# Strassen operands of an encoder layer: transposing the four plain blocks and forming the sums from transposed blocks

## The chip, the core and the metric

The kernel runs on one core of one Trainium2 chip. The metric is the device time of one execution in microseconds (us); the time of a kernel is the median over several runs. The engines of the core are named PE (TensorE, matmul; its weight loads are PEld), DVE (VectorE), ACT (ScalarE), POOL (GpSimd) and SP (SyncE). SBUF is the core's working memory, PSUM the small memory into which PE writes.

## The reference

One layer of an encoder: 1024 tokens, width 1024, float32 in and out.

```
x += 1/2 * post(SwiGLU_1(pre(x)))                      macaron half-step FFN
x += post(W_out [ norm(NA heads) | norm(dilated heads) ])  parallel head groups
     sharing one combined q/k/v projection of pre(x)
x += 1/2 * post(SwiGLU_2(pre(x)))                      macaron half-step FFN
...
def swiglu(x, w_gate, w_up, w_down):
    return (jax.nn.silu(x @ w_gate) * (x @ w_up)) @ w_down
```

`pre` and `post` are root-mean-square norms with a gain. The hidden width of the two SwiGLU networks is 2816. The large products have pre(x) on the left: the gates and ups of ffn1, q/k/v, and the gates and ups of ffn2.

## The kernel before

**Products.** Each float32 operand is split into a high and a low part of a shorter format (`fp32r`): hi is a cast on ACT, lo is the difference on DVE. A product is then three matmuls (`mm3`, L251 to L253). Above this lies one level of Strassen's scheme in Winograd's form: the left operand, pre(x) transposed, is cut into four blocks of 512x512, and seven products are made of the left blocks and sums A11, S2, S1, S4, A12, S3, A22 with the right ones (B and T). The left sums are S1 = A21 + A22, S2 = S1 - A11, S3 = A11 - A21, S4 = A12 - S2.

**The left operands.** The class `Operand` makes these seven in three places of the program: before ffn1, before the q/k/v projection and before ffn2. The tokens come in eight tiles of 128. Of tiles 0 to 3 come A11 (left half of the columns) and A12 (right half); of tiles 4 to 7 come A22, S1, S2, S3 and S4, whose sums take tile t and tile t-4. For each tile, `squares` sums the squares (ACT, L151), `scale` makes the factor on DVE (L134 to L144) and `tile` writes the normalised tile `xn` (L200). Tiles 0 to 3 are saved to memory by a DMA of POOL (L203) and loaded again as `x1` (L217) when their partner is in work. `sums` forms the four sums in the natural layout into `s` (L223). Each of the 28 pieces of a place then goes through `transpose_in`: four transposes on PE into `trp` (L159; two PSUM buffers), the cast hi by ACT (L160) and the subtraction lo by DVE (L161).

**Buffers.** `xn` has 3 buffers at ffn1 and 2 at the other places (`c.xn`); `x1` and `s` have 2 at ffn1 and 1 at the others (`c.deep`). In the last two places `squares` uses the next `xn` buffer as its throw-away output, so it too waits for that buffer.

**What sets the order.** The pieces are fed in between the matmuls of another product: after every six matmuls, `Ctx.step` takes one entry of `c.sums` (norms and sums) and one of `c.steps` (a piece); what is left is done in a row by `flush`. PE keeps this order as it is written. ACT and DVE keep it only at the head of ffn1; elsewhere a scheduler sets the order of ACT, DVE, POOL and SP. During ffn1 and ffn2 the pieces lie between the first products of the gate and up weights, which need A11 and A12 alone ("early" pairs: 9 at ffn1, 10 at ffn2; their weights `graw` are split into `whi` and `wlo`, L344 and L345). Then `begin` prepares the right operands of the first pair: `traw` (T2) and `wraw` are weight sums (L432 to L434, DVE), split at L344 and L345; the first product of the run of all seven is S2 x T2. In the early pairs `sg` is the activated product (L528, ACT), `s` at L363 the kept copy of the A11 product. At the q/k/v projection the pieces for tiles 4 to 7 lie within the product for v, whose output is copied to `vt` (L1357) and whose weights are cast at L600. The residual stream x is read and written by POOL's DMAs at L705 and L709 between the norms.

Of the kernel before, what the change touches and what calls it, by code (L numbers as in the profile page):

```python
# [10 lines left out]
F32 = mybir.dt.float32  # L11
# [8 lines left out]
P, T = 128, 512  # L20
# [8 lines left out]
A11, S2, S1, S4, A12, S3, A22 = range(7)  # L29
# [124 lines left out]
def transpose_in(c, x, hi, lo, tag="tr", pool=None):  # L154

    nc = c.nc
    ps = (pool or c.pst).tile([P, 4, P], F32, tag=tag, name="trp")
    for j in range(4):
        nc.tensor.transpose(ps[:, j, :], x[:, j * P:(j + 1) * P], c.ident)  # L159
    nc.scalar.copy(hi, ps)  # L160
    nc.vector.tensor_sub(lo, ps, hi.bitcast(F32))  # L161


class Operand:
# [9 lines left out]
    def second(self):  # L174
        for b in (S1, S2, S3, S4, A22):
            self.x[b] = [self.c.xb.tile([P, 4, T], F32R, tag=f"x{b}{i}", name=f"x{b}{i}") for i in range(2)]
# [19 lines left out]
    def tile(self, t, x, xn, r):  # L196
        c, nc = self.c, self.c.nc
        if xn is None:
            xn = c.xp.tile([P, D], F32, tag="xn", name="xn", bufs=c.xn)
        nc.vector.scalar_tensor_tensor(xn, x, r, self.gain, op0=ALU.mult, op1=ALU.mult)  # L200
        a1, a2 = xn[:, :T], xn[:, T:]
        if t < 4:
            nc.gpsimd.dma_start(self.saved[t], xn)  # L203
            self.parts[t] = deque(((A11, a1), (A12, a2)))
        else:
            self.wait.append((t, a1, a2))
            self.sums()

    def sums(self):

        c, nc = self.c, self.c.nc
        if not self.wait or self.open == c.deep:
            return
        self.open += 1
        t, a1, a2 = self.wait.popleft()
        x1 = c.xp.tile([P, D], F32, tag="x1", name="x1", bufs=c.deep)
        nc.gpsimd.dma_start(x1, self.saved[t - 4])  # L217
        s = c.xp.tile([P, 4, T], F32, tag="s", name="s", bufs=c.deep)
        a11, a12 = x1[:, :T], x1[:, T:]
        s1, s2, s3, s4 = [s[:, i, :] for i in range(4)]  # L220
        add, sub = nc.vector.tensor_add, nc.vector.tensor_sub
        for f, *args in ((add, s1, a1, a2), (sub, s2, s1, a11), (sub, s3, a11, a1), (sub, s4, a12, s2)):
            c.sums.append(lambda f=f, args=args: f(*args))  # L223
        parts = deque(((A22, a2), (S1, s1), (S2, s2), (S3, s3), (S4, s4)))
        c.sums.append(lambda: self.parts.__setitem__(t, parts))

    def put(self, t):

# [3 lines left out]
    def one(self, t):  # L232
        while not self.parts.get(t):
            self.c.sums.popleft()()
        b, src = self.parts[t].popleft()
        cols = slice(t % 4 * P, t % 4 * P + P)
        transpose_in(self.c, src, *[h[:, :, cols] for h in self.x[b]])
        if t >= 4 and not self.parts[t]:
            self.open -= 1
            self.sums()  # L240
# [82 lines left out]
class PairGemm:  # L323
# [17 lines left out]
    def split(self, raw, tag, pool=None):  # L341
        c, nc = self.c, self.c.nc
        hi, lo = [(pool or c.wr).tile(list(raw.shape), F32R, tag=tag + p, name="w" + p) for p in ("hi", "lo")]
        nc.scalar.copy(hi, raw)  # L344
        nc.vector.tensor_sub(lo, raw, hi.bitcast(F32))  # L345
        return hi, lo
# [73 lines left out]
    def prepare(self, b):  # L420


        nc = self.c.nc
        if b >= self.n:
            return [lambda: None] * 4
        r, w = self.raw.pop(b), self.w.setdefault(b, {})
        t2 = self.c.wt.tile([P, 1, T], F32, tag="t", name="traw")

        def direct():
            if b >= self.early:  # L430
                w["g"] = self.split(r[:, 0:4:3, :], "g")
            nc.vector.tensor_sub(r[:, 0:2], r[:, 1:3], r[:, 0:2])  # L432
            nc.vector.tensor_sub(t2[:, 0], r[:, 2], r[:, 0])  # L433
            nc.vector.tensor_sub(r[:, 3], r[:, 3], t2[:, 0])  # L434

        def second():
            w[T2] = self.split(t2, "t", self.c.wt)

        def sums():
            w[T1] = self.split(r[:, 0:2, :], "m")  # L440

        def rest():
            w[B22] = self.split(r[:, 2:4, :], "n")
            self.fetch(b + 2)
        return direct, second, sums, rest
# [11 lines left out]
    def run(self, final=None):  # L457
# [3 lines left out]
        for b in range(self.n):  # L461
            w, early = self.w.pop(b), b < self.early
            direct, second, sums, rest = self.prepare(b + 1)
            if early:
                s1 = sp.tile([P, T], F32, tag="s1", name="s1")
# [30 lines left out]
            c22 = c.cp.tile([P, T], F32, tag="g2", name="c22", bufs=3)  # L496
            nc.vector.tensor_add(c22, d, v)
            sums()
            self.mm(a, w[B22], 0, S4, True)
            self.sink.second(b, a, u2 if early else None)  # L500
# [13 lines left out]
class GatePairs:  # L514
# [7 lines left out]
    def first(self, b, ps, keep, s1=None):  # L522
        c, nc = self.c, self.c.nc
        sg = c.sp.tile([P, T], F32, tag="s1", name="sg") if keep else self.tile()
        if s1 is not None:
            nc.vector.tensor_add(sg, ps, s1)
            ps = sg
        nc.scalar.activation(sg, ps, AF.Silu)  # L528
        self.sg[b] = sg
        if keep:  # L530
            self.sg[b] = d = c.dr.tile([P, T], F32, name="sgd")
            nc.gpsimd.dma_start(d, sg)
# [133 lines left out]
class Finish:  # L666
# [33 lines left out]
    def rest(self, ts, h):  # L700

        c, nc = self.c, self.c.nc
        xs = [c.xp.tile([P, D], F32, tag="x", name="x") for t in ts]
        for t, x in zip(ts, xs):
            nc.gpsimd.dma_start(x, self.src[t])  # L705

        def add(t, x):
            nc.vector.scalar_tensor_tensor(x, h(t), self.r[t], x, op0=ALU.mult, op1=ALU.add)
            nc.gpsimd.dma_start(self.dst[t], x)  # L709
        c.sums.extend([lambda: None] * 2 + [lambda t=t, x=x: add(t, x) for t, x in zip(ts, xs)])  # L710
        if self.op is not None:
            c.sums.append(lambda: self.op.norm(ts, xs))
# [884 lines left out]
```

## Time and profile before

| what | value |
|---|---|
| time, median of 3 runs | 1975.63 us (1974.63 to 1976.17) |
| profiled execution | span 1973.4 us; the page shows no other time for it |
| granted TensorE clock, mean | 0.977 |
| traffic to and from memory | 203 GB/s over the span |

The rows of five stretches show the three places. Columns: start and end, length, busy us and count of PE, PEld, DVE, ACT and POOL, the granted clock (1.00 is full speed), the busy share of the DMA engines and GB/s.

```profile
50.00:75.00 25.00, 25.00 (x134) 20.65 (x134) 23.43 (x43) 15.18 (x25) 4.87 (x9) 1.00 0.58 194
85.40:100.00 14.60, 13.54 (x65) 11.02 (x64) 8.96 (x12) 6.95 (x11) 2.16 (x4) 1.00 0.90 351
635.00:725.00 90.00, 84.72 (x390) 67.77 (x389) 72.51 (x132) 44.40 (x73) 15.64 (x29) 1.00 0.70 244
1300.00:1345.00 45.00, 39.55 (x182) 31.67 (x181) 33.32 (x63) 25.58 (x40) 10.26 (x19) 0.95 0.83 299
1345.00:1376.00 31.00, 27.29 (x122) 22.04 (x121) 21.26 (x36) 11.76 (x20) 3.76 (x7) 0.85 0.40 137
```

In the first PE never stops; in the last two, at ffn2, it stands for 5.45 us of 45 and 3.71 us of 31, and the clock is below full speed. In the timeline a row is start, duration, engine, line, operation, tiles, and in brackets the idle time before it with what released it.

### The profile page before, as it was taken

The page shows a single profiled execution, that of the slowest core. Times are in us where ns is not written, and L with a number is a line of the kernel's source. Part 1 is how long each engine was busy: PE and PEld are TensorE (multiplying, and loading weights), DVE is VectorE, ACT ScalarE, POOL GpSimd, SP SyncE. Part 2 cuts the span into 40 slices and gives each one's busy share as a digit, 9 for nine tenths or more (in the row PEclk, how much of TensorE's full clock was granted, in tenths as well). Part 3 has the DMA queues.
Part 4 walks back from the last instruction along what each step waited for, and adds up shares of the span by engine and source line. Part 5 has one row for each costly group of instructions (what it writes and reads, how often), then busy time and mean ns, then how long its engine had stood idle before and what let it go on. Part 6 is the DMA issues. An engine that isn't in the chain of part 4 may idle for free. (4 is left out here: it accounts for less than half of the span.)

```text
span 1973.4 us, 25565 instructions
## 1 busy us (share of the span) xinstructions
PE 1878.4 (95%) x9044; PEld 1566.3 (79%) x9044; DVE 1329.0 (67%) x2235; ACT 807.0 (41%) x1463; POOL 323.3 (16%) x520
## 2 busy tenths in 40 slices
PE   5999999999999989999899788998999999999997
PEld 4888888887888868778898777876888888878886
DVE  5778776764656775577565565676788777745567
ACT  4522233333534455133676555454222333335333
POOL 2101111111000123323444220021011111110000
PEclk8999999999999999999999799998999999999999
DMA  6655565555876767868999881375456665467664
GB/s 234 216 170 176 180 231 203 202 192 208 292 251 204 255 232 254 243 214 244 207 190 159 144 164 32 132 271 193 160 178 204 234 225 192 172 220 234 202 220 143
DMA packets 170433, 398.63 MB, mean 202 GB/s; under 512 B 20080, under 2 KB 41504, under 8 KB 170304
## 3 DMA queue, kind: packets, MB, share of 16 engines
q1 hardware_dynamic: 118800, 222.34, 36.1%
q0 software_dynamic: 50640, 172.55, 27.6%
q10 hardware_dynamic: 864, 2.10, 0.3%
q8 instruction: 71, 1.16, 0.2%
q14 instruction: 58, 0.48, 0.1%
HBM read 272.55 MB, written 127.26 MB: 203 GB/s over the span
## 5 line engine op out<-in xcount | busy, mean ns | idle before, releaser
L251 PE MATMUL mmp<-x,whi 128*128 128x512 f32 (+1 forms) x1464 | 580.9, 397 | 7.6 <-ACT whi L344 3.5
L253 PE MATMUL mmp<-x,wlo 128*128 128x512 f32 (+1 forms) x1464 | 576.5, 394 | 1.1 <-DVE wlo L345 1.1
L252 PE MATMUL mmp<-x,whi 128*128 128x512 f32 (+1 forms) x1464 | 576.1, 394 | 0.6 <-DVE x L161 0.5
L251 PEld LDWEIGHTS mmp<-x,whi 128*128 128x128 f32 x1464 | 278.8, 190 | 67.4 <-ACT whi L344 4.2
L253 PEld LDWEIGHTS mmp<-x,wlo 128*128 128x128 f32 x1464 | 278.7, 190 | 62.2 <-DVE wlo L345 1.9
L252 PEld LDWEIGHTS mmp<-x,whi 128*128 128x128 f32 x1464 | 278.9, 191 | 59.8 <-DVE x L161 1.5
L601 DVE TENSOR_TENSOR pw<-praw,pw 128x1024 fp32r<-128x1024 f32 (+1 forms) x182 | 198.9, 1139 | 128.1 <-ACT pw L600 128.0
L600 ACT CAST pw<-praw 128x1024 fp32r<-128x1024 f32 (+1 forms) x182 | 168.4, 981 | 215.6 <-PE accp L253 173.5
L252 PE MATMUL accp<-pw 128*128 128x512 f32 x616 | 241.7, 392 | 4.9 <-DVE pw L601 4.9
L251 PE MATMUL accp<-pw 128*128 128x512 f32 x616 | 241.9, 393 | 2.6 <-ACT pw L600 2.6
L253 PE MATMUL accp<-pw 128*128 128x512 f32 x616 | 241.2, 391 | 0.0
L344 ACT CAST whi<-wraw 128x1024 fp32r<-128x1024 f32 x129 | 135.3, 1050 | 248.6 <-PE mmp L252 223.2
L345 DVE TENSOR_TENSOR wlo<-wraw,whi 128x1024 fp32r<-128x1024 f32 x129 | 157.7, 1224 | 23.8 <-ACT whi L344 23.6
L252 PEld LDWEIGHTS accp<-pw 128*128 128x128 f32 x616 | 116.4, 189 | 30.1 <-DVE pw L601 6.4
L251 PEld LDWEIGHTS accp<-pw 128*128 128x128 f32 x616 | 116.4, 189 | 27.5 <-ACT pw L600 3.5
L253 PEld LDWEIGHTS accp<-pw 128*128 128x128 f32 x616 | 116.4, 189 | 24.2
L549 POOL DMA_DIRECT2D g<-sg x44 | 23.8, 540 | 473.3 <-DVE sg L542 285.8
L363 ACT COPY s<-mmp 128x512 f32<-128x512 f32 x52 | 30.5, 586 | 149.8 <-PE mmp L253 148.1
L505 DVE TENSOR_TENSOR c<-mmp,u 128x512 f32<-128x512 f32 x52 | 35.9, 691 | 81.2 <-PE mmp L253 80.9
L161 DVE TENSOR_TENSOR x<-trp,x 128x512 fp32r<-128x512 f32 x84 | 57.2, 687 | 35.6 <-ACT x L160 35.6
L344 ACT CAST whi<-traw 128x512 fp32r<-128x512 f32 x52 | 32.3, 621 | 117.1 <-DVE traw L433 58.4
L432 DVE TENSOR_TENSOR wraw<-wraw 128x1024 f32<-128x1024 f32 x52 | 63.7, 1224 | 23.5 <-DMA wraw<-in_wqk_dram 12.6
(223 smaller groups left out, 2760.9 us busy)
## 6 DMA issues: line engine op xcount, KB each, us to landing
praw<-g SPq DMA_DIRECT2D x70, 512.0 KB
wraw<-in_wg_dram SPq DMA_DIRECT2D x44, 512.0 KB
wraw<-in_wu_dram SPq DMA_DIRECT2D x44, 512.0 KB
tr<-in_wd_dram SPq DMA_DIRECT2D x44, 512.0 KB
g<-sg POOLq DMA_DIRECT2D x88, 256.0 KB, 3.4
ts<-tr POOLq DMA_DIRECT2D x22, 1024.0 KB, 4.7
praw<-ts SPq DMA_DIRECT2D x88, 256.0 KB
praw<-in_wd_dram SPq DMA_DIRECT2D x66, 256.0 KB
```

What stands on the lines that cost most here:

```text
L161: nc.vector.tensor_sub(lo, ps, hi.bitcast(F32))
L251: nc.tensor.matmul(out, ahi, bhi, start=start, stop=False, skip_group_check=go_on)
L252: nc.tensor.matmul(out, ahi, blo, start=False, stop=False, skip_group_check=go_on)
L253: nc.tensor.matmul(out, alo, bhi, start=False, stop=stop, skip_group_check=go_on)
L344: nc.scalar.copy(hi, raw)
L345: nc.vector.tensor_sub(lo, raw, hi.bitcast(F32))
L363: self.c.nc.scalar.copy(s, ps)
L432: nc.vector.tensor_sub(r[:, 0:2], r[:, 1:3], r[:, 0:2])
L505: nc.vector.tensor_add(c21, d, u2)
L549: nc.gpsimd.dma_start(self.g[A12 if b % 2 else A11][b // 2], g)
L600: nc.scalar.copy(w[:, side, 0, :m], raw[:, :m])
L601: nc.vector.tensor_sub(w[:, side, 1, :m], raw[:, :m], w[:, side, 0, :m].bitcast(F32))
```

## The change

Only plain blocks are transposed: A11 and A12 of tiles 0 to 3, A22 and A21 (the two halves) of tiles 4 to 7. A place has 16 groups of four transposes in place of 28. A transposed block is copied back by ACT over the half of `xn` that it came from, so that `xn` then holds transposed blocks; the save of tiles 0 to 3 comes after the second half's copy, and `x1` is loaded transposed. The sums are formed from transposed blocks: S1 and S3 read A21 from PSUM, S2 and S4 read SBUF; their hi and lo are split from `s` in SBUF. A tile of the second half is now five steps: `right` (transpose A22, split, copy back), `left` (transpose A21, S1 and S3), `first` (split S1, form S2), `second` (split S2, form S4), `rest` (split S4 and S3). The number of DVE's operations and of DMAs stays as it is; ACT has 12 copies more per place. Lines behind `Operand` stand 39 further down.

```diff
--- before.py
+++ after.py
@@ -198,13 +198,35 @@
         if xn is None:
             xn = c.xp.tile([P, D], F32, tag="xn", name="xn", bufs=c.xn)
         nc.vector.scalar_tensor_tensor(xn, x, r, self.gain, op0=ALU.mult, op1=ALU.mult)
-        a1, a2 = xn[:, :T], xn[:, T:]
         if t < 4:
-            nc.gpsimd.dma_start(self.saved[t], xn)
-            self.parts[t] = deque(((A11, a1), (A12, a2)))
+            self.parts[t] = deque([lambda: self.plain(t, xn, 0, A11), lambda: self.plain(t, xn, 1, A12)])
         else:
-            self.wait.append((t, a1, a2))
+            self.wait.append((t, xn))
             self.sums()
+
+    def cols(self, t, b):
+        return [h[:, :, t % 4 * P:t % 4 * P + P] for h in self.x[b]]
+
+    def split(self, t, b, src):
+        nc = self.c.nc
+        hi, lo = self.cols(t, b)
+        nc.scalar.copy(hi, src)
+        nc.vector.tensor_sub(lo, src, hi.bitcast(F32))
+
+    def turned(self, xn, half):
+
+        c, ps = self.c, self.c.pst.tile([P, 4, P], F32, tag="tr", name="trp")
+        for j in range(4):
+            c.nc.tensor.transpose(ps[:, j, :], xn[:, half * T + j * P:half * T + j * P + P], c.ident)
+        return ps, xn[:, half * T:half * T + T].rearrange("p (k c) -> p k c", k=4)
+
+    def plain(self, t, xn, half, b):
+
+        ps, back = self.turned(xn, half)
+        self.split(t, b, ps)
+        self.c.nc.scalar.copy(back, ps)
+        if half:
+            self.c.nc.gpsimd.dma_start(self.saved[t], xn)
 
     def sums(self):
 
@@ -212,17 +234,36 @@
         if not self.wait or self.open == c.deep:
             return
         self.open += 1
-        t, a1, a2 = self.wait.popleft()
+        t, xn = self.wait.popleft()
         x1 = c.xp.tile([P, D], F32, tag="x1", name="x1", bufs=c.deep)
         nc.gpsimd.dma_start(x1, self.saved[t - 4])
-        s = c.xp.tile([P, 4, T], F32, tag="s", name="s", bufs=c.deep)
-        a11, a12 = x1[:, :T], x1[:, T:]
-        s1, s2, s3, s4 = [s[:, i, :] for i in range(4)]
+        s = c.xp.tile([P, 4, 4, P], F32, tag="s", name="s", bufs=c.deep)
+        a11, a12 = [x1[:, i * T:i * T + T].rearrange("p (k c) -> p k c", k=4) for i in range(2)]
+        s1, s2, s3, s4 = [s[:, i] for i in range(4)]
         add, sub = nc.vector.tensor_add, nc.vector.tensor_sub
-        for f, *args in ((add, s1, a1, a2), (sub, s2, s1, a11), (sub, s3, a11, a1), (sub, s4, a12, s2)):
-            c.sums.append(lambda f=f, args=args: f(*args))
-        parts = deque(((A22, a2), (S1, s1), (S2, s2), (S3, s3), (S4, s4)))
-        c.sums.append(lambda: self.parts.__setitem__(t, parts))
+
+        def right():
+            ps, back = self.turned(xn, 1)
+            self.split(t, A22, ps)
+            nc.scalar.copy(back, ps)
+
+        def left():
+            ps, _ = self.turned(xn, 0)
+            add(s1, ps, xn[:, T:].rearrange("p (k c) -> p k c", k=4))
+            sub(s3, a11, ps)
+
+        def first():
+            self.split(t, S1, s1)
+            sub(s2, s1, a11)
+
+        def second():
+            self.split(t, S2, s2)
+            sub(s4, a12, s2)
+
+        def rest():
+            self.split(t, S4, s4)
+            self.split(t, S3, s3)
+        self.parts[t] = deque((right, left, first, second, rest))
 
     def put(self, t):
 
@@ -232,9 +273,7 @@
     def one(self, t):
         while not self.parts.get(t):
             self.c.sums.popleft()()
-        b, src = self.parts[t].popleft()
-        cols = slice(t % 4 * P, t % 4 * P + P)
-        transpose_in(self.c, src, *[h[:, :, cols] for h in self.x[b]])
+        self.parts[t].popleft()()
         if t >= 4 and not self.parts[t]:
             self.open -= 1
             self.sums()
```

How the built orders move, at three places. First ACT at the end of the early pairs of ffn1; the line L344 (L383 after the change) casts weights, L160 (L213) casts the left operands, L528 (L567) is the activation of an early product. Before:

```order
L160 CAST x_177<-trp 128x4x128
L160 CAST x_179<-trp 128x4x128
L363 COPY s_885<-mmp 128x512
L528 ACTIVATE sg<-mmp 128x512
L344 CAST whi<-traw 128x512
L528 ACTIVATE sg<-mmp 128x512
L344 CAST whi<-wraw 128x1024 x2
L344 CAST whi<-traw 128x512
L344 CAST whi<-wraw 128x1024
```

The same place with the change:

```order
L213 CAST x_173<-s 128x4x128
L213 CAST x_177<-s 128x4x128
L213 CAST x_175<-s 128x4x128
L402 COPY s_837<-mmp 128x512
L213 CAST x_179<-s 128x4x128
L567 ACTIVATE sg<-mmp 128x512 x2
L383 CAST whi<-wraw 128x1024
L383 CAST whi<-traw 128x512
```

The two casts of weights have changed places, and both now stand behind the last two activations, where the cast of `traw` stood between them.

Second POOL at the head of the norms of ffn2; L203 (L229) saves the normalised tile, L705 and L709 (L744 and L748) read and write the residual stream, L217 (L239) loads a saved tile again. Before:

```order
L705 DMA x<-x_2_95 128x1024
L705 DMA x<-x_3_96 128x1024
L203 DMA xn_0_10909<-xn 128x1024
L203 DMA xn_1_10910<-xn 128x1024
L709 DMA x_2_103<-x 128x1024
L709 DMA x_3_104<-x 128x1024
L217 DMA x_11580<-xn_0_10909 128x1024
L203 DMA xn_2_10911<-xn 128x1024
```

With the change:

```order
L744 DMA x<-x_2_95 128x1024
L744 DMA x<-x_3_96 128x1024
L748 DMA x_2_103<-x 128x1024
L748 DMA x_3_104<-x 128x1024
L229 DMA xn_0_10813<-xn 128x1024
L229 DMA xn_1_10814<-xn 128x1024
L239 DMA x_11492<-xn_0_10813 128x1024
L744 DMA x<-x_4_97 128x1024
L744 DMA x<-x_5_98 128x1024
L229 DMA xn_2_10815<-xn 128x1024
L229 DMA xn_3_10816<-xn 128x1024
```

The saves of tiles 0 and 1 have moved behind the two writes of x, and those of tiles 2 and 3 behind two reads.

Third DVE at the second half of the tiles of ffn2; L432 (L471) is the first weight sum of `begin`, which waits for a weight's DMA, L134 starts the norm of the next two tiles. Before:

```order
L161 TENSOR_TENSOR x_11429<-trp,x_11428 128x4x128
L223 TENSOR_TENSOR s<-s,x_11728 128x512
L223 TENSOR_TENSOR s<-x_11728,xn 128x512
L223 TENSOR_TENSOR s<-x_11728,s 128x512
L161 TENSOR_TENSOR x_11431<-trp,x_11430 128x4x128
L134 TENSOR_SCALAR v<-ss 128x2
L432 TENSOR_TENSOR wraw<-wraw 128x1024
L135 TENSOR_SCALAR y<-v 128x2
L161 TENSOR_TENSOR x_11423<-trp,x_11422 128x4x128
L136 TENSOR_SCALAR y<-y 128x2
L345 TENSOR_TENSOR wlo<-graw,whi 128x1024
```

With the change:

```order
L214 TENSOR_TENSOR x_11343<-trp,x_11342 128x4x128
L471 TENSOR_TENSOR wraw<-wraw 128x1024
L252 TENSOR_TENSOR s<-trp,xn 128x512
L253 TENSOR_TENSOR s<-x_11626,trp 128x512
L257 TENSOR_TENSOR s<-s,x_11626 128x512
L214 TENSOR_TENSOR x_11335<-s,x_11334 128x4x128
L384 TENSOR_TENSOR wlo<-graw,whi 128x1024
L261 TENSOR_TENSOR s<-x_11626,s 128x512
L214 TENSOR_TENSOR x_11337<-s,x_11336 128x4x128
L134 TENSOR_SCALAR v<-ss 128x2
```

Before, the four sums of tile 5 stood ahead of L432; now all four and a low half of early weights stand behind it.

## The prediction

> **What bounds the kernel now.** I read the page first, then the groups of the trace that touch the tile `trp`, then the order of time around each place where the operands are made.
>
> ```profile
> span 1973.4 us, 25565 instructions
> PE 1878.4 (95%) x9044; PEld 1566.3 (79%) x9044; DVE 1329.0 (67%) x2235; ACT 807.0 (41%) x1463; POOL 323.3 (16%) x520
> ```
>
> PE is busy for 95% of the span, and the other engines have room on average. So an instruction taken from PE shortens the span by its own length, unless PE then reaches something that is not ready. The question is which of the two happens at each of the three places (before ffn1, before the q/k/v projection, before ffn2).
>
> ```profile
> L159 PE MATMUL trp<-ident,s x192: 269/272/477, 53.3 to 1371.0; 128*128 128x128 f32 x192
> L159 PE MATMUL trp<-ident,xn x144: 270/273/475, 11.9 to 1365.3; 128*128 128x128 f32 x144
> ```
>
> These are the transposes: 192 of sums, 144 of plain blocks. The durations (min, median, max in ns) overlap in the pipeline, so the price is read from the starts:
>
> ```profile
> 53.29 0.60 PE L159 MATMUL trp<-ident,s 128*128 128x128 f32 x4
> ...
> 55.14 0.60 PE L159 MATMUL trp<-ident,s 128*128 128x128 f32 x4
> ...
> 1376.30 0.40 PE L251 MATMUL mmp<-x,whi 128*128 128x512 f32 x1
> ...
> 1377.68 0.40 PE L251 MATMUL mmp<-x,whi 128*128 128x512 f32 x1
> ```
>
> From one group of four to the next, with six matmuls after the first, PE takes 55.14 - 53.29 = 1.85 us; six matmuls alone take 1377.68 - 1376.30 = 1.38 us. A group costs 0.47 us; over several such pairs I take **0.45 us**.
>
> **What the change removes.** Per place, tiles 0 to 3 keep 2 groups each; tiles 4 to 7 fall from 5 groups to 2. That is 28 groups before and 16 after, 12 fewer: 12 x 0.45 = **5.4 us per place, 16.2 us in all**. ACT gets 12 copies back from `trp` per place, of about 0.57 us, and DVE does as many subtractions as before:
>
> ```profile
> L160 ACT CAST x<-trp x84: 565/586/605, 13.8 to 1371.5; 128x512 fp32r<-128x512 f32 x84
> L161 DVE TENSOR_TENSOR x<-trp,x 128x512 fp32r<-128x512 f32 x84 | 57.2, 687 | 35.6 <-ACT x L160 35.6
> L223 DVE TENSOR_TENSOR s<-xn x12: 680/686/693, 47.9 to 1363.5; 128x512 f32<-128x512 f32 x12
> ```
>
> A subtraction that reads PSUM takes 687 ns, a sum in SBUF 686 ns: where the operand lies changes nothing, so the work that moves between them is costed at nothing. The 36 copies are 36 x 0.57 = 20 us of ACT; PE covers them, except where a cast that PE waits for stands behind one. I now follow the changed orders place by place.
>
> **Place 1 (ffn1).** Five transposes in a flush before the last early pair made PE wait, and this wait goes:
>
> ```profile
> 87.50 0.66 PE L159 MATMUL trp<-ident,s 128*128 128x128 f32 x4 [1.06 <-DVE x L161]
> 93.82 0.60 ACT L528 ACTIVATE sg<-mmp 128x512 f32<-128x512 f32 x1 [2.19 <-PE mmp L253]
> 94.31 0.61 ACT L344 CAST whi<-traw 128x512 fp32r<-128x512 f32 x1
> 96.61 0.60 ACT L528 ACTIVATE sg<-mmp 128x512 f32<-128x512 f32 x1 [1.69 <-issue]
> 97.11 1.99 ACT L344 CAST whi<-wraw 128x1024 fp32r<-128x1024 f32 x2
> ```
>
> What is late next is the product S2 x T2, which starts without a wait at 96.37. Its T2 cast stands between the last two activations of `sg` and is done at 94.92. In the changed order ACT does both activations, then the 1024-wide cast, and only then T2's. The last `sg` waits for the matmuls that end just ahead of the product, so PE waits for the tail of it (0.50), a 1024-wide cast (1.05, less 0.1 of overlap) and T2's cast (0.62): 2.1 us. The low half then needs two subtractions on DVE, and its matmul comes about 1.0 later: -3.1 in all. At the head of the program a copy back stands ahead of the second cast (0.5), and the fourth `xn` (3 buffers) now waits for the save of tile 0, which the diff puts behind the copy back of the second half. The save starts near 22.8, and
>
> ```profile
> DMA to landing us min/median/max: 2.9/4.1/7.0
> 27.46 0.56 POOL L203 DMA_DIRECT2D xn<-xn  x1 [7.88 <-DVE xn L200]
> ```
>
> the first row (landing of the saves) puts it at 26.9, where this `xn` was written just before its save at 27.46: no slack, 0.3. After a wait the clock can fall:
>
> ```profile
> 1339.73 0.40 PE L253 MATMUL mmp<-x,wlo 128*128 128x512 f32 x1
> 1343.24 0.66 PE L159 MATMUL trp<-ident,s 128*128 128x128 f32 x4 [3.12 <-DVE x L161]
> ...
> 1344.38 0.63 PE L253 MATMUL mmp<-x,wlo 128*128 128x512 f32 x1
> 1344.81 0.63 PE L251 MATMUL mmp<-x,whi 128*128 128x512 f32 x1
> 722.53 0.50 PE L251 MATMUL mmp<-x,whi 128*128 128x512 f32 x1 [1.66 <-ACT whi L344]
> 1344.00:1348.00 4.00, 4.00 (x14) 3.23 (x13) 3.76 (x13) 1.69 (x3) 0.54 (x1) 0.58 0.35 131
> ```
>
> After a wait of 3.12 us the matmuls are 0.43 apart in place of 0.23, for about eight of them: 8 x 0.20 = 1.6 us lost, at a granted clock of 0.58; the wait of 1.66 us is followed by a matmul of 0.50, near the usual 0.40 and far from 0.63. A wait of 3.1 in two parts lies between: 0 to 1.6, I take 1.0. **Place 1: 5.4 + 1.06 - 3.1 - 0.8 - 1.0 = +1.6 us.**
>
> The Trainium skill, "TensorE: Matmul & The Clock Gate", Part 1, says that the gate halves the clock after an idle window of about 3.4 us, and that the window runs free of the kernel. The rows above agree for 3.12 (0.58) and for 1.66. Taken strictly, a wait in two parts of 2.1 and 1.0 never empties a window, and the sum would be 1.0 better.
>
> **Place 2 (q/k/v).** Here the flush stands at the end of V's product:
>
> ```profile
> 715.13 0.66 PE L159 MATMUL trp<-ident,s 128*128 128x128 f32 x4 [0.67 <-DVE x L161]
> 720.95 0.59 ACT L1357 COPY vt<-accp 128x512 f32<-128x512 f32 x1 [0.85 <-PE accp L253]
> 721.43 1.99 ACT L344 CAST whi<-graw 128x1024 fp32r<-128x1024 f32 x2
> ```
>
> The 0.67 goes. PE then stands at 722.53 (row above) for `whi`, which ACT casts behind the last `vt` copy. In the changed order the last tile's casts of S3 and S4 stand ahead of these, so of the 2.0 us that PE saves on the last tiles (4.4 groups) only 0.7 arrives: -1.3. The first weight cast of V's S2 pass is moved behind the activation of another tile: bounds 0 and the 2.0 of two casts (1.99 above), I take 1.0, the middle, as no row is nearer. Cold clock: 0 to 1.6, I take 0.5. **Place 2: 5.4 + 0.67 - 1.3 - 1.0 - 0.5 = +3.3 us.**
>
> **Place 3 (ffn2).** Here the old kernel waits longest, and the new one gets new waits.
>
> ```profile
> 1364.90 0.63 PE L159 MATMUL trp<-ident,xn 128*128 128x128 f32 x4 [1.48 <-DVE x L161]
> ...
> 1367.81 1.96 PE L159 MATMUL trp<-ident,s 128*128 128x128 f32 x8 [1.69 <-DVE x L161]
> 1370.31 1.12 PE L159 MATMUL trp<-ident,s 128*128 128x128 f32 x4 [0.55 <-DVE x L161]
> PE trp L159 <- DVE x L161: 8.3, 6, 3.1
> ```
>
> With the 3.12 these waits are 6.84 us, and all are for the two buffers of `trp`, which a cast and a subtraction free; sums hold none now. The cold clock behind them costs 1.6 after 1343.24, as much after 1371, and 12 transposes at half speed some 1.4 (1.96 for eight where 1.03 is usual): 4.6. So 5.4 + 6.84 + 4.6 = +16.8 gross. Against it:
>
> ```profile
> 1279.90 1.06 POOL L203 DMA_DIRECT2D xn<-xn  x2
> 1286.58 0.53 POOL L709 DMA_DIRECT2D x<-x  x1 [2.19 <-DVE x L708]
> 1286.26 1.06 ACT L151 ACTIVATE xn<-x 128x1024 f32<-128x1024 f32 x1 [3.63 <-DMA xn<-xn]
> 1288.96 0.17 DVE L134 TENSOR_SCALAR v<-ss 128x2 f32<-128x2 f32 x1 [0.35 <-ACT xn L151]
> 1292.28 2.48 DVE L200 SCALAR_TENSOR_TENSOR xn<-x,y,gain 128x1024 f32<-128x1024 f32 x2
> 1294.28 0.60 PE L159 MATMUL trp<-ident,xn 128*128 128x128 f32 x4
> 1341.29 1.23 DVE L432 TENSOR_TENSOR wraw<-wraw 128x1024 f32<-128x1024 f32 x1 [3.78 <-DMA wraw<-in_wu_dram]
> ```
>
> *Save loop.* `xn` has 2 buffers: the squares of tiles 2 and 3 (ACT, 1286.26) already wait for the saves issued at 1279.90. The changed order puts these saves behind POOL's write of x_3 (1286.58) and behind the copies back: 1287.1 and 1288.7, plus 4.1 to land; the second squares end near 1294, the chain from 1288.96 to 1292.28 adds 3.3, the scaling 1.3: tile 2 stands near 1298.2, and PE wants it at 1294.28. -3.9, and cold clock -1.0.
>
> *DVE behind a weight.* L432 holds DVE until 1341.3 for a DMA. In the changed order all sums of tile 5 stand behind it, and behind these a low half of early weights (`wlo<-graw`), so PE still waits there, for the weights now: 0 to 3.78, I take the middle less the slack of a group, 1.9 - 0.2 = 1.7. Tile 5's last use of `xn` comes as much later, and the squares of tile 7 wait for that buffer: -1.9.
>
> *The last reload.* x1 has one buffer, and is free only after S4 of tile 6.
>
> ```profile
> DMA to landing us min/median/max: 4.0/5.6/9.1
> ```
>
> So the sums of tile 7 come 5.6 us (landing of the reloads) behind the last of tile 6, with only two groups and the products of one pair over it; the weight sums, T2's cast and its low half follow behind them on DVE and ACT: hi 4.3 late, lo 1.3 more: -5.6, cold clock -2.0. The bounds of this term are 0 (the products of the last pair hide it) and 9.1. **Place 3: 16.8 - 4.9 - 3.6 - 7.6 = +0.7 us.**
>
> Sum: 1.6 + 3.3 + 0.7 = 5.6. The profiled execution's span is 1973.4, so 1967.8 after; no time around it is shown, and the median of the runs (1975.63) lies 2.2 above it, which I keep: **1970.0 us**.
>
> **Rivals.** *R1, the new waits stay hidden*: ACT has 59% of the span free and DVE 33%, and if the scheduler's orders leave the weight casts early enough, all of 16.2 arrives: 1975.6 - 16.2 = 1959.4. Against it are the orders of ACT at place 1 and of POOL at place 3. *R2, the waits eat it all*: at place 3 the save loop and the last reload at their longest (7.0 and 9.1 in place of 4.1 and 5.6) cost 6.4 more: 1976.4, no change. For it speaks that each old wait for `trp` was a wait for DVE, and DVE loses nothing. *R3, slower*: the hold of `xn` until its save has landed, in all three places. If the saves take 7.0, the 0.2 of slack at places 1 and 2 goes and each place waits 2.7 to 2.9 more: 8.3, and each new wait passes into the cold clock, 3 x 1.6 = 4.8: 1983.1. It turns slower (over 1979.6) from a landing of about 5.7. Against it: the median is 4.1. That the change does not do what it says is excluded: the built order has 144 transposes fewer.
>
> **How the numbers follow.** Forecast 0.48, own range 1964.5 to 1972; R1 0.16; R2 0.27; R3 0.09. A measurement of this kernel tells some 0.2% (4 us) from no change, so faster means below 1971.7. The forecast's upper end crosses it a little: faster 0.62, same 0.29, slower 0.09. The range takes in R1 and the most of R2: 1959 to 1977.5.
>
> **What would show it.** At place 1, a wait of PE at the first S2 product for a T2 cast of 2 us or more; at place 3, transposes of tile 2 that wait for `xn`, DVE idle for the last reload, and no wait of `trp` for its subtraction. A median under 1962 would say that the waits did not come; a place 2 that gains less than 1 would say that V's casts cost more than bounded.

## The result, and the profile after

The change made the kernel slower. In the first comparison the median was 1984.28 us (1979.81 to 1989.25, 6 runs) against 1975.13 us before; ratio 1.0055, 95% interval 1.0037 to 1.0072. A second comparison (e5 below) gave 1978.47 against 1973.17, ratio 1.0020, interval 1.0006 to 1.0035. Both intervals lie above 1, so the sign is the same in both; the size is 0.2 or 0.55%, and the two intervals do not meet. The forecast was 1970.0 and faster.

The head of the page of the changed kernel:

```profile
span 1978.0 us, 25332 instructions
PE 1868.0 (94%) x8900; PEld 1551.8 (78%) x8900; DVE 1328.6 (67%) x2235; ACT 827.0 (42%) x1499; POOL 323.2 (16%) x520
```

PE has its 144 transposes less (9044 to 8900) and 10.4 us less of busy time, ACT 36 copies more. Yet the span is 4.6 us longer: what PE no longer does, it waits. The groups of the left-operand matmuls say for what:

```profile
L290 PE MATMUL mmp<-x,whi 128*128 128x512 f32 (+1 forms) x1464 | 579.7, 396 | 19.2 <-ACT whi L383 10.4
L292 PE MATMUL mmp<-x,wlo 128*128 128x512 f32 (+1 forms) x1464 | 578.0, 395 | 5.8 <-DVE wlo L384 5.8
```

The same two groups before:

```profile
L251 PE MATMUL mmp<-x,whi 128*128 128x512 f32 (+1 forms) x1464 | 580.9, 397 | 7.6 <-ACT whi L344 3.5
L253 PE MATMUL mmp<-x,wlo 128*128 128x512 f32 (+1 forms) x1464 | 576.5, 394 | 1.1 <-DVE wlo L345 1.1
```

The last part is the idle time before the matmuls and the releaser of most of it: 7.6 us before and 19.2 now for the first matmul of three, 1.1 and 5.8 for the third.

To see where it is lost, I set each matmul's start in one trace against the same matmul's start in the trace of before (the transposes left out). The difference is the delay up to that point; its change over a stretch is what the stretch lost (+) or won (-), in us. Times are those of before:

```
stretch                      change  change again (e5)
place 1  0 to 48             +2.15   +2.68
         48 to 95            -5.07   -5.02
         95 to 118           +4.91   +4.91
place 2  640 to 770          -1.18   -0.86
place 3  1270 to 1306        +8.60   +7.16
         1306 to 1374        -13.0   -9.67
         1374 to 1395        +7.98   +6.96
the three places             +4.4    +6.2
the rest                     +0.3    +7.0
```

The gain is there (48 to 95, 1306 to 1374) and is given back at two kinds of place: the first S2 x T2 product of each FFN, and the first normed tiles of ffn2. The losses repeat within 1.5 us from trace to trace. The rest, untouched by the change, moves by several us from one trace to the next (waits for transfers in the value product, the attention and the down products), and this is why a single trace settles a stretch but not the span. All differences are against one trace of before, which has accidents of its own: from 118 to 640 all twelve other traces of this document are 1.0 to 3.5 us ahead of it, and from 770 to 960 eleven of the twelve fall behind it, by 0.9 to 6.6.

**Place 1, S2 x T2.** PE, then ACT, in the order of time:

```profile
93.21 0.40 PE L292 MATMUL mmp<-x,wlo 128*128 128x512 f32 x1
95.80 0.50 PE L290 MATMUL mmp<-x,whi 128*128 128x512 f32 x1 [2.19 <-ACT whi L383]
96.13 0.40 PE L291 MATMUL mmp<-x,whi 128*128 128x512 f32 x1
97.14 0.74 PE L292 MATMUL mmp<-x,wlo 128*128 128x512 f32 x1 [0.61 <-DVE wlo L384]
97.68 0.63 PE L290 MATMUL mmp<-x,whi 128*128 128x512 f32 x1
98.11 0.63 PE L291 MATMUL mmp<-x,whi 128*128 128x512 f32 x1
```

```profile
93.69 0.60 ACT L567 ACTIVATE sg<-mmp 128x512 f32<-128x512 f32 x1 [2.21 <-PE mmp L292]
94.19 1.04 ACT L383 CAST whi<-wraw 128x1024 fp32r<-128x1024 f32 x1
95.12 0.62 ACT L383 CAST whi<-traw 128x512 fp32r<-128x512 f32 x1
```

This is the wait that the prediction worked out (2.1 us and about 1.0): 2.19 and 0.61, and then eight matmuls 0.43 apart, at the halved clock. But T2's sum is late as well, which the prediction did not have:

```profile
85.41 0.65 SPq L377 DMA_DIRECT2D wraw<-in_wg_dram  x1
```

```profile
92.19 1.23 DVE L471 TENSOR_TENSOR wraw<-wraw 128x1024 f32<-128x1024 f32 x1 [2.28 <-DMA wraw<-in_wu_dram]
93.45 0.69 DVE L472 TENSOR_TENSOR traw<-wraw 128x512 f32<-128x512 f32 x1
```

The first of these transfers in the trace of before:

```profile
82.38 0.66 SPq L338 DMA_DIRECT2D wraw<-in_wg_dram  x1
```

It is issued 3.0 us later now, though PE is ahead by 2.9 us at the end of this stretch. The trace says what it waits for: the first of these transfers waited 9.9 us for transposes of PE (L159) before, and waits 13.0 us for DVE's sums (L253) now. By the program the weights are loaded over the memory in which the last tiles and sums stand, and these are read until later now, since the sums come after the transposes.

**Place 2, the same loop.** At q/k/v a tile of `xn` is waited for too, where nothing was before:

```profile
679.41 0.63 PE L220 MATMUL trp<-ident,xn 128*128 128x128 f32 x4 [1.14 <-DVE xn L200]
```

**Place 3, the save loop.** PE, then POOL, then ACT:

```profile
1281.25 0.66 PE L220 MATMUL trp<-ident,xn 128*128 128x128 f32 x4 [1.35 <-ACT xn L227]
...
1284.99 0.66 PE L220 MATMUL trp<-ident,xn 128*128 128x128 f32 x4 [1.68 <-ACT xn L227]
...
1296.35 1.08 PE L220 MATMUL trp<-ident,xn 128*128 128x128 f32 x4 [3.88 <-DVE xn L200]
...
1307.95 0.51 PE L290 MATMUL mmp<-x,whi 128*128 128x512 f32 x1 [2.79 <-ACT xn L227]
```

```profile
1285.23 0.53 POOL L229 DMA_DIRECT2D xn<-xn  x1 [0.68 <-ACT xn L227]
1287.90 0.53 POOL L229 DMA_DIRECT2D xn<-xn  x1 [2.14 <-ACT xn L227]
```

```profile
1280.61 0.59 ACT L227 COPY xn<-trp 128x512 f32<-128x512 f32 x1 [1.48 <-DVE x L214]
...
1290.89 1.06 ACT L151 ACTIVATE xn<-x 128x1024 f32<-128x1024 f32 x1 [0.68 <-DMA xn<-xn]
```

The wait for `xn` is 3.88 us where 3.9 were forecast. What was not forecast is that PE waits for the copy back (L227), which itself waits for DVE. The row at 1280.61 shows it: ACT stands idle for 1.48 us until DVE's low half has read `trp`. Of the 24 copies of this line, 18 wait for DVE's subtraction, 16.1 us together. Cast, subtraction and copy read the same PSUM tile (`trp`) one after another. So a buffer of `trp` is free only after three operations, and the saves start later by one of them. The same places in the trace of before:

```profile
1284.23 0.66 PE L159 MATMUL trp<-ident,xn 128*128 128x128 f32 x4 [0.84 <-DVE x L161]
1286.94 0.66 PE L159 MATMUL trp<-ident,xn 128*128 128x128 f32 x4 [0.67 <-DVE x L161]
...
1302.17 0.50 PE L251 MATMUL mmp<-x,whi 128*128 128x512 f32 x1 [1.82 <-ACT whi L344]
1303.43 0.80 PE L253 MATMUL mmp<-x,wlo 128*128 128x512 f32 x1 [0.52 <-DVE wlo L345]
```

So PE waited at the same two transposes before, for the subtraction, and the copy adds 0.5 and 1.0 us to these waits. The wait of 2.79 us is that of the first early product, which stood before too, for its weights (1.82 and 0.52); it adds only 0.3 net. The 8.6 us are these 1.5 and 0.3, about 4.0 of the wait for `xn`, and 2.7 of half clock behind it: the granted clock from 1296 to 1302 is 0.50, and four transposes take 1.08 us in place of 0.66.

**Place 3, the middle.** The stretch from 1306 to 1374 wins, but one new wait stands in it:

```profile
1346.85 1.23 DVE L471 TENSOR_TENSOR wraw<-wraw 128x1024 f32<-128x1024 f32 x1 [5.30 <-DMA wraw<-in_wu_dram]
1351.66 0.50 PE L292 MATMUL mmp<-x,wlo 128*128 128x512 f32 x1 [3.03 <-DVE wlo L384]
```

This is the low half of early weights that now stands on DVE behind the weight sum, which waits for its DMA, and the sums of tile 5, as the prediction says. Between 1350 and 1354 on the clock of before, it costs 3.3 us in this trace and 7.7 in the second (a wait of 4.76), which is why the second wins 3.4 us less there.

### The profile page after: what moved, and what is told of

Same layout as the page of the kernel before. It is cut to its first block, busy times and chain, and to the rows that moved or that the text cites. A ratio compares the mean times of both kernels' runs of the same rounds, so it can differ in the third digit from the quotient of the medians.

```text
span 1978.0 us, 25332 instructions
## 1 busy us (share of the span) xinstructions
PE 1868.0 (94%) x8900; PEld 1551.8 (78%) x8900; DVE 1328.6 (67%) x2235; ACT 827.0 (42%) x1499; POOL 323.2 (16%) x520
## 4 chain that ended last, share of the span: by engine, by line
PE 78%; DVE 8%; DMA 5%; issue 4%; ACT 3%; POOL 1%; SPq 1%; DVEq 0%; ACTq 0%; POOLq 0%
PE mmp L292 16%; PE mmp L290 15%; PE mmp L291 15%; PE accp L291 8%; PE accp L290 8%; PE accp L292 8%; PE po L990 2%; PE ptp L896 2%; PE po L1090 1%; PE sp L970 1%; DMA vs<-v 1%; DMA praw<-in_wd_dram 1%; PE sp L1073 1%; DVE x L214 1%; DVE pw L640 1%
## 5 line engine op out<-in xcount | busy, mean ns | idle before, releaser
L290 PE MATMUL mmp<-x,whi 128*128 128x512 f32 (+1 forms) x1464 | 579.7, 396 | 19.2 <-ACT whi L383 10.4
L383 ACT CAST whi<-wraw 128x1024 fp32r<-128x1024 f32 x129 | 135.4, 1050 | 249.1 <-PE mmp L291 221.0
L383 ACT CAST whi<-traw 128x512 fp32r<-128x512 f32 x52 | 32.3, 621 | 127.1 <-PE mmp L291 66.7
L471 DVE TENSOR_TENSOR wraw<-wraw 128x1024 f32<-128x1024 f32 x52 | 63.6, 1224 | 26.1 <-DMA wraw<-in_wu_dram 15.1
L1090 PEld LDWEIGHTS po<-vs,pt 128*128 128x128 f32 x352 | 50.5, 206 | 10.8 <-DVE pt L898 4.3
```

The costliest lines, as they stand in the source:

```text
L290: nc.tensor.matmul(out, ahi, bhi, start=start, stop=False, skip_group_check=go_on)
L1090: nc.tensor.matmul(po[0][:, u], pt[0][:, j, :], vs[:, k0 + j, f], start=j == 0, stop=j == n - 1)
```

## Experiments

Each kernel was timed against the kernel before in five rounds, in three sets on one chip each; ratios are to the kernel before in the same set. "Place" means the stretches of the table above.

**e1 to e3: the change at one place alone.** The class of before is kept as `OperandB` and used at the other two places:

```diff
-            op0 = Operand(c, load_gain(c, a["ffn1_pre_g"], "pre"), 0)
+            op0 = OperandB(c, load_gain(c, a["ffn1_pre_g"], "pre"), 0)
...
-            op = Operand(c, g3, 2)
+            op = OperandB(c, g3, 2)
```

(shown for e2, which keeps the change at the q/k/v projection alone; e1 and e3 likewise). Expected:

> The change at ffn1 alone; the operands of q/k/v and ffn2 are made as before. Theory T (the loss sits in new waits at the end of places 1 and 3): +2.0 us against before, with a wait of some 2.2 and 0.6 us ahead of the first S2 x T2 product and cold matmuls behind it, and a gain of 5 us up to that point. Rival W (the loss is the added work of ACT, spread evenly): a third of the loss of 9 us, +3, without one place where it arises. Rival V (the loss is an accident of transfers elsewhere): -3.5, the share of the removed transposes less the head.

> The change at the q/k/v projection alone. T: about -1 us (the groups gone, 5.3 us, less a wait of 3.3 in place of 1.7 for the first weights, 1.1 for xn and some 1.5 at the low halves of the weights of v). W: +3. V: -4.

> The change at ffn2 alone. T: +3.6 us: 8.6 lost between the first transposes and the tile that waits for xn, 14 won from there to the last early pair, 8.3 lost at the first S2 x T2 product. W: +3. V: -5.

Measured: e1 1984.64 (ratio 1.0053, 1.0036 to 1.0069), e2 1976.51 (1.0002, 0.9984 to 1.0021), e3 1978.96 (1.0025, 1.0009 to 1.0041), against 1974.47. In the traces place 1 lost 4.2 us in e1, with 4.9 at S2 x T2 again; place 3 lost 2.9 in e3 (+6.7, -11.8, +8.0); place 2 won 1.5 in e2. So places 1 and 3 lose and place 2 is level, as T says, and V, which has gains at all three, falls. W's +3 lies within the interval of e2; against an evenly spread loss speak the traces, in which the loss arises at a few waits. But e1's +10 us is more than place 1 shows in its trace: the untouched stretch from 770 to 960 lost 5 us there, and 4.4 to 6.3 in e2 and e3 as well, whose medians are far lower. By their medians the three add to 16.7 us, more than the whole change lost in either comparison (9.2 and 5.3). What the rest of e1 is stays open.

**e4: the low half reads the copy.** Expected:

> All three places as in the change, but ACT copies a plain block back right behind its cast, and DVE's low half reads the copy in SBUF in place of trp, so that trp is read by ACT alone. If part of the loss comes from trp being held by three readers one after another (cast, subtraction, copy), the waits of PE for the copy at ffn2 (1.35, 1.68 and 2.79 us) go, the saves start 0.7 us earlier per half, and the time falls by 4 to 7 us against the change: 1977 to 1980. If only the save's landing and the order of the T2 cast matter, it falls by 0 to 1.5: 1983 to 1984.

```diff
         nc.scalar.copy(hi, src)
+        if back is not None:
+            nc.scalar.copy(back, src)
+            src = back
         nc.vector.tensor_sub(lo, src, hi.bitcast(F32))
```

(the copies behind `split` go, and `back` is handed to it). Measured: 1977.72, ratio 1.0010 (0.9993 to 1.0027), 6.6 us below the first median of the change and 0.8 below the second; by medians alone the gain is not shown. Two rows of ACT and one of PE at ffn2, in e4:

```profile
1278.79 0.59 ACT L213 CAST x<-trp 128x512 fp32r<-128x512 f32 x1 [0.74 <-PE trp L223]
1279.27 0.59 ACT L215 COPY xn<-trp 128x512 f32<-128x512 f32 x1
```

```profile
1295.16 1.08 PE L223 MATMUL trp<-ident,xn 128*128 128x128 f32 x4 [5.93 <-DVE xn L200]
```

The copy now follows its cast at once and ACT waits for PE alone. The waits of PE for the copy are gone: none is left at the transposes of tiles 0 and 1, and the first early product waits for its weights again (2.31 and 0.50). PE is sooner at the tile that waits for `xn` and waits there longer, 5.93 in place of 3.88. By the traces the edit wins 1.2 us from 48 to 95 (-5.9 to -6.5 in the five traces that have it, -4.8 to -5.1 in the five of kernels that change place 1 without it), and 2.9 to 4.4 us at place 3 as a whole: 0.0 in e4 (+6.5, -12.0, +5.5) against +3.6 and +4.4 in the change's two traces and +2.9 in e3. Together that is some 4 to 5 us. In the save loop itself nothing can be read: 6.5 lost, and 5.9 to 8.6 in the traces without the edit (the change twice, e3, e9), since what the copies held up before is now waited for at `xn`. In e4 the head to 48 was 2.6 better too, but in the other four kernels with the edit it is not. So the serial reading of `trp` was a cost of its own, at the lower end of the 4 to 7 that I expected; the two large losses (4.9 at S2 x T2 of ffn1, 6.5 in the save loop) stay.

**e5: the change again.**

> The changed kernel once more, for a second time and a second trace. If the losses are in the order of the program, place 1 loses 2 to 4 us against before, place 3 loses 3 to 5, place 2 gains 1 to 2, each wait within 1 us of the first trace. If they are accidents of transfers, they move.

The table above shows it: every loss and gain at the places is found again, within 1.5 us except the middle of place 3, where 3.4 us less were won. Place 1 lost 2.6 (2 to 4 expected) and place 3 4.4 (3 to 5); place 2 won 0.9, just under the 1 to 2 expected. The rest moved by 7 us.

**e6: e4 with the T2 cast in its old order.**

> The kernel of e4 (low half from the copy) with the T2 cast of the first pair put ahead of the last activation of the early pairs again, as it stands in the kernel before; the other first casts stay behind that activation. If this order makes the wait at the first S2 x T2 product of ffn1 (4.9 us with its cold matmuls in all three traces that have it), it goes at ffn1, where T2's sum is ready at 88.6 and PE arrives at 89.5; at ffn2, where the sum itself is late, 1 us is won. Together -5 to -6 us against e4: 1972. If the weights' transfers, issued some 3 us later than before, are the cause, at most 1 us is won: 1977.

```diff
         if ready:
-            c.behind(self.begin, DVE, ACT)
-        late()
+            with c.tc.manual_schedule(engines={mybir.EngineType.PE, ACT}):
+                c.behind(self.begin, DVE, ACT)
+                late()
+        else:
+            late()
...
-            pg.begin_rest()
+            c.behind(pg.begin_rest, ACT)
```

Measured: 1967.89, ratio 0.9971 (0.9957 to 0.9984); -7.7 us against e4 by the two ratios. ACT at the end of the early pairs of ffn1, in e6:

```profile
88.98 0.60 ACT L571 ACTIVATE sg<-mmp 128x512 f32<-128x512 f32 x1 [2.22 <-PE mmp L293]
90.65 0.62 ACT L384 CAST whi<-traw 128x512 fp32r<-128x512 f32 x1 [1.07 <-DVE traw L476]
91.74 0.60 ACT L571 ACTIVATE sg<-mmp 128x512 f32<-128x512 f32 x1 [0.47 <-PE mmp L293]
92.23 1.99 ACT L384 CAST whi<-wraw 128x1024 fp32r<-128x1024 f32 x2
```

T2 is cast between the two activations, and PE does not wait: 0.6 us lost from 95 to 118 in place of 4.9. At ffn2 the stretch from 1374 lost 2.6 in place of 5.5, three times what I had expected there. The order of one cast of 0.62 us is worth 4.3 us at ffn1.

**e7: e4 without the squares in the `xn` buffers.**

> The kernel of e4, but the squares of tiles 0 to 3 are written to the idle buffer of the sums (as ffn1 does at its head) and not to the xn buffers, so that the norm of tiles 2 and 3 no longer waits for the saves of tiles 0 and 1; only their scaling does. If the save loop makes the loss of 6.5 us at ffn2 (and the 1 us at q/k/v), PE's wait of 5.9 us for xn falls to about 1.5 and the cold matmuls go: -5 us against e4: 1972.5. If PE waits there for the order of the residual stream's work, nothing changes: 1977.7.

```diff
-        n = self.squares(ts, xs)
+        c = self.c
+        junk = c.xp.tile([P, D], F32, tag="s", name="junk", bufs=c.deep) if ts[0] < 4 else None
+        n = self.squares(ts, xs, junk)
```

Measured: 1968.57, ratio 0.9976 (0.9962 to 0.9990). PE at the same tile of ffn2, in e7:

```profile
1288.57 0.66 PE L225 MATMUL trp<-ident,xn 128*128 128x128 f32 x4 [0.53 <-ACT xn L217]
...
1295.92 0.60 PE L225 MATMUL trp<-ident,xn 128*128 128x128 f32 x4
```

No wait for the normed tile is left, better than the 1.5 us expected: from 1270 to 1306 the trace won 0.5 where e4 lost 6.5. The loop ran through the throw-away output of the squares: the norm of tiles 2 and 3 could not begin before the transposed tiles 0 and 1 had landed in memory. About half of the gain is lost again further on, at the early products and the wait for `wlo` in the middle (4.26 us here, 3.49 in e4): place 3 as a whole is 3.3 us better than in e4. At q/k/v the loss at `xn` goes as well (1.5 us in e4, nothing in e7), but the first product behind waits longer, and the place as a whole wins 0.3, not the 1 expected.

**e8: both.**

> e6 and e7 together. If the two causes are apart, the gains add: -10 us against e4, 1967, and faster than the kernel before by 0.3%. If one wait only hands over to the next, the sum is smaller: 1971 to 1974.

Measured: 1965.32 (6 runs), ratio 0.9951 (0.9935 to 0.9968); 12.4 us below e4 by the medians and 11.6 by the ratios, where 10 were expected. At the two stretches both causes are apart: in the trace of e8 the delay grows by 0.3 at S2 x T2 of ffn1 and falls by 0.7 in the save loop, in one kernel. In the whole time the gains fall short of adding up: e6 and e7 alone are 7.7 and 6.7 us below e4 by the ratios, together 14.4.

**e9 and e10: one thing undone in the change itself** (the edits of e6 and e7 alone).

> The changed kernel with one thing undone: the T2 cast ahead of the last activation, nothing else (the low half still reads trp). If the order of the cast were all, the loss at the first S2 x T2 product of ffn1 would fall from 4.9 to 0.5 us as in e6. But the weights are asked for 3.0 us later here than in the kernel before (85.4 in place of 82.4) and T2's sum is ready only 0.9 us after PE arrives, so I expect a wait of 1.3 to 1.6 us to stay, 2 to 2.5 with the low half and the clock: a gain of 2.5 there and 2 at ffn2, together 4 to 5 us against the change.

> The changed kernel with the squares of tiles 0 to 3 in the idle buffer of the sums, nothing else. The save loop at ffn2 (7.2 to 8.6 us lost between 1270 and 1306) falls to 1 to 3 us: the waits for trp's copy stay. Gain 5 to 7 us against the change, nothing at ffn1. If trp's three readers were the main cause of the loss there, the gain is under 2.

Measured: e9 1977.49 (1.0016, 1.0000 to 1.0032), e10 1977.66 (1.0014, 0.9998 to 1.0029), against 1974.75. At S2 x T2 of ffn1 e9 loses 1.6 in place of 4.9, with this wait left:

```profile
94.94 0.50 PE L290 MATMUL mmp<-x,whi 128*128 128x512 f32 x1 [1.03 <-ACT whi L383]
```

That is the part of the later weights: ACT waits for T2's sum there, and DVE for the weight's DMA (2.01 us). A wait of 1.3 to 1.6 and a loss of 2 to 2.5 had been expected. At ffn2, where 2 us were expected, the stretch from 1374 loses 6.7 in place of 8.0 and 7.0. In e10 the save loop loses 3.3 in place of 7.2 to 8.6 (1 to 3 expected), with waits of 1.86 and 1.50 for the copy left. The ratios put both 0.04 to 0.4% under the change, since the change's own two values differ; by the whole times alone neither gain is shown.

**e11: e8 with two buffers for the tile loaded again at ffn2.**

> The kernel of e8 with a second buffer for the tile loaded again (x1) at ffn2; the sums' buffer is taken when the sums are formed. If the last reload (asked for only after S4 of tile 6) makes S2 x T2 of ffn2 late, the 4.2 us lost there in e8 fall to 1 to 2 and the time to 1962 to 1963. If the buffer was not the cause but DVE's row of sums and low halves is, the loss stays at 3.5 to 4.5 and the time at 1965.

```diff
-        x1 = c.xp.tile([P, D], F32, tag="x1", name="x1", bufs=c.deep)
+        x1 = c.xp.tile([P, D], F32, tag="x1", name="x1", bufs=c.x1)
...
-        if not self.wait or self.open == c.deep:
+        if not self.wait or self.open == max(c.deep, c.x1):
...
+            s4 = c.xp.tile([P, 4, 4, P], F32, tag="s", name="s", bufs=c.deep)
```

(the throw-away output of ffn2's other squares also goes to the sums' buffer, to make room). DVE in e8, then PE in e8, then PE in e11, at the last tile of ffn2:

```profile
1358.16 0.68 DVE L255 TENSOR_TENSOR s<-trp,xn 128x512 f32<-128x512 f32 x1
1360.39 0.69 DVE L256 TENSOR_TENSOR s<-x,trp 128x512 f32<-128x512 f32 x1 [1.55 <-DMA x<-xn]
```

```profile
1367.26 0.79 PE L293 MATMUL mmp<-x,whi 128*128 128x512 f32 x1 [2.79 <-ACT whi L386]
```

```profile
1372.98 0.50 PE L294 MATMUL mmp<-x,whi 128*128 128x512 f32 x1 [1.20 <-ACT whi L387]
```

With the second buffer DVE no longer waits for the load, PE waits 1.20 in place of 2.79, and the stretch loses 1.3 in place of 4.2. Measured: 1961.99 (1958.06 to 1970.41, 8 runs), ratio 0.9936 (0.9915 to 0.9957). The time is 3.3 us below e8, with intervals that overlap; the stretch shows the cause. This is the fastest of the kernels and beats both before and the change: the idea wins 0.6% once most of its new waits are taken away. The wait for `wlo` in the middle of place 3 is still there (3.93 us).

## Why the prediction was wrong, point by point

The forecast has the three places win 5.6 us; in the first trace they lose 4.4. The 10.0 us between are 1.4 at the head, 1.4 up to 95, 0.8 at S2 x T2 of ffn1, 2.1 at place 2, 3.7 in the save loop, 0.2 in the middle of place 3 and 0.4 at its end.

- **The price of the transposes** was right. Where nothing else moves, each missing group brings the matmuls 0.43 to 0.45 us forward. The middle of place 3 (13.2 forecast from the gone groups, waits and cold clock less the weight that holds DVE) won 13.0 and 9.7; the weight's term, 3.6, came out at 3.3 and 7.7, and in the second trace its wait of 4.76 lies beyond the bound of 3.78.
- **"The 36 copies are 20 us of ACT; PE covers them"** is the step that failed. The copies were priced as load of ACT, and the sum has them only in the later saves and with 0.5 at the head; their cost is also that they hold `trp` behind the subtraction, and with it the next transposes. e4 takes the hold away and wins 4 to 5 us by the traces, 1.2 of them at place 1. The trace of before gave the sign: PE waits 0.84 and 0.67 us for `trp` at tiles 0 and 1 of ffn2, two of the six waits in the row "8.3, 6, 3.1", of which the prediction used the other four; the third reader was put behind just these. This step is not all of it: e4 is still no faster than before, and the half clock was undersized by 2.4 us (0.7 at place 1, 1.7 in the save loop).
- **Place 1**: +1.6 forecast, -2.0 and -2.6 measured. S2 x T2 cost 4.9 where 4.1 was forecast (mechanism right, shown by e6; some 1 us of it is the weights asked for later, shown by e9, which the prediction lacked). The stretch to 95 won 5.1 where 6.5 stood, and e4 wins 1.2 of that back. The head cost 2.15 where 0.8 stood; kernels with the old head differ there by -2.1 and +0.4 from the trace of before, no experiment took it apart, and its cause stays open.
- **Place 2**: +3.3 forecast, +1.2 and +0.9 measured, on the edge of the sign that the prediction set (a gain under 1), and not for the reason given there alone. PE waits for `xn` in the changed kernel, 1.14 and 1.69 us in its two traces, where 0.2 of slack were assumed; with the squares out of the way (e7, e8, e10, e11) nothing is lost there. The first weights cost about what was forecast (3.33 in place of 1.66). Behind them the clock falls, 1.4 us; but it does so too in e1 and e3, which keep the old place 2 and differ from before by +2.1 and +1.4 us. So against these the gain is 2 to 3 us, and the trace of before was lucky there.
- **Place 3**: +0.7 forecast, -3.6 and -4.4 measured. The save loop was sized at 4.9 and cost 8.6 and 7.2: the longer waits for `trp` and more half clock came on top. That the wait for `xn` was right to 0.1 us is luck: both saves were issued sooner than forecast (1285.2 and 1287.9, not 1287.1 and 1288.7) and landed in 3.2 us (the median), not 4.1, and PE came 1.8 us sooner too. The last reload with S2 x T2 was sized at 7.6 and cost 8.0 and 7.0; e6 and e11 show its two parts, the order of the casts and the single buffer.
- **The cold clock.** I took 1.0 of 0 to 1.6 after a wait in two parts at place 1; it was 1.7. After the wait for `xn` I took 1.0 again, and it was 2.7 in the first trace. The Trainium skill, "TensorE: Matmul & The Clock Gate", Part 1, speaks of an idle window of about 3.4 us; here 2.19 and 0.61 us with two matmuls between them were enough, so the strict reading, under which the sum would have been 1.0 better, did not hold. The prediction's own row of 3.12 us, which it counted as agreeing, is shorter than 3.4 as well.
- **The rivals.** In time R3 (1983.1) is nearest to the first comparison and R2 (1976.4) to the second, but neither for its reason: both have the transfers at their longest (7.0 for a save), and the saves of the changed kernel landed in 3.2 us, 5.6 at most. R3 had the right sign and the right loop; what stands before the save decided, not a long landing.
- **The range** rested on one trace for each term. Stretches that the change does not touch moved by up to 7 us between two traces of one kernel.

## What to carry to other kernels

An operation added to a "free" engine is not priced by that engine's idle share but by what it holds: here a PSUM buffer, a tile waiting to be saved, and a place in the queue ahead of a cast that the next stage needs first. When work is taken off the bounding engine, look at the first thing that engine needs next at each stage's end, and make its producers early by hand; a cast of 0.62 us in the wrong place cost seven times its length here (4.3 us). Take a reader away from the shared buffer (let the second engine read the copy) before taking away work.

## What was not expected of the hardware

The clock fell after waits of 2.19 and 0.61 us in place 1, and all six traces with that order lost the same 4.9 us. It did not fall in e9 after 1.03 us: matmuls stay 0.23 apart there. The length of a wait alone does not decide: after 1.66 and 0.55 us at 722.5 the clock stayed up in the trace of before, and after the same two waits at the same matmuls it fell in e1 and in e3. In e1:

```profile
725.48 0.50 PE L369 MATMUL mmp<-x,whi 128*128 128x512 f32 x1 [1.66 <-ACT whi L462]
726.76 0.50 PE L371 MATMUL mmp<-x,wlo 128*128 128x512 f32 x1 [0.55 <-DVE wlo L463]
...
728.61 0.63 PE L371 MATMUL mmp<-x,wlo 128*128 128x512 f32 x1
729.03 0.63 PE L369 MATMUL mmp<-x,whi 128*128 128x512 f32 x1
```

These are 0.42 us apart, and the fall costs 1.5 us. What makes the difference no run here shows. The waits of 2.8 us in place 1 cost 4.9 us, less the 0.3 to 0.8 that the same stretch loses without them (e8, e6, e11). One kernel's runs on one chip spread by up to 1.0% (e2: 1970 to 1989), with single stretches that depend on transfers moving by 2 to 5 us and more; differences of 0.2% needed the comparison of the same matmul in two traces beside the medians.
